# First mixture of experts: rows fetched by number from DRAM instead of by one-hot products, and a ring of 8 weight buffers instead of 6

## Chip, cores and metric

The kernel runs on 1 core of one Trainium2 chip. The metric is device time in microseconds (us) of one execution: 2,796.69 us before, the median of 3 runs (2,793.19 to 2,798.8).

## What is computed

Two blocks run one after the other: a transformer block (SwiGLU, attention, SwiGLU), and a second block of two layers, each with a mixer (gMLP, then RWKV) and a mixture of experts over 32 experts, 2 for each token. The first mixture works on 512 tokens, the second on 256. Cut to the mixture, the reference is:

```python
def hier_moe(h, w_grp, b_grp, w_exp, b_exp, w_gate, w_up, w_down):
    grp = jnp.argmax(grp_logits, axis=-1)               # best of 4 groups
    top_logit, top_idx = lax.top_k(exp_logits, TOP_K)   # 2 of its 8 experts
    weights = (p_grp * jax.nn.softmax(top_logit, axis=-1)).astype(h.dtype)
    ...
    def expert_block(args):
        xb, e = args
        return (jax.nn.silu(xb @ w_gate[e]) * (xb @ w_up[e])) @ w_down[e]
    ...
    return jnp.einsum('tk,tkd->td', weights, y)
```

All of it is float32. An expert has three matrices of 1024x512 (gate, up, down), 2 MiB each; both mixtures read all 32 experts.

## The kernel before

`moe` (L759) does a mixture. It opens a ring of weight buffers of 16 KiB a partition (`more_ring`, L771: 6 of them in the first mixture, l = 0), normalises the tokens into `h` (features down the partitions), computes the router's logits and lets `route` number the slots: expert e owns slots 64 e to 64 e + 63, and `dl` holds, token by token, the slot of its first and of its second expert. `h` is transposed tile by tile on TensorE, and the rows are kept in SBUF in two parts, `ht` high and low, whose sum is the float32 value (L808 to L811). `DB` and `WB` are slot numbers and weights of all tokens, spread over all partitions (L817, L819).

`experts` (L995) then makes 16 steps of 2 experts, 128 slots a step. Step q has these parts on TensorE:

- the gather (`gather`, L916): VectorE builds one-hot matrices `oh` of this step's slots (L923, L924), TensorE multiplies them with `ht`: 4 token tiles, 2 parts and 2 halves are 16 products `px<-hth,oh` and `px<-htl,oh` (L932); ScalarE copies the sum to `Xs` (L933); 8 transposes (L938) and 2 copies (L939) make `X`, features down;
- gate and up (L1010): 16 matmuls each, two experts side by side in the two column halves of the array; TensorE shows each float32 matmul as two records;
- `takers` and `hidden`: VectorE finds each slot's weight (L949 to L952), silu on ScalarE (L959), the product on VectorE (L960), 4 transposes (L963), a copy `hT` (L965);
- down in two halves b (L1030), 8 matmuls each, whose result is split into `y` high and low by ScalarE (L987) and VectorE (L988);
- `combine` (L974): 16 matmuls scatter `y` back to the 512 tokens, and VectorE adds them into the residuals `Rl` and `Rc` (L977): 8 feature tiles, 2 updates each, through 2 PSUM buffers `pc`.

The gather of step q + 1 is written behind gate and up of step q, but which instruction stands where on an engine is decided by a scheduler with its own estimate of times. SP issues the weights' loads in the order gate, up, down, two buffers each; a load waits until TensorE is through with what its buffer held before. `extra` (L1037) is a loop over further slots of experts with more than 64 tokens; no instruction of its body appears in the trace. Behind the first mixture stand the RWKV mixer and the second mixture (l = 1, 8 steps of 4 experts).

Of the kernel before, what the change touches and what calls it, by code (L numbers as in the profile page):

```python
# [222 lines left out]
class K:  # L223
# [529 lines left out]
    def moe(self, R, l, n, rs):  # L753

        nc, i, v = self.nc, self.i, self.nc.vector
# [11 lines left out]
        nt = n // 128  # L767
        with ExitStack() as es:

            if not l:  # L770
                es.enter_context(self.more_ring(6))  # L771
            pool = es.enter_context(self.tc.tile_pool(name=self.uid("moe"), bufs=1))
            if l:
                es.enter_context(self.more_ring(6, before=self.rings))
            ht = [pool.tile([128, nt, D], F32R, name=f"ht{j}") for j in "hl"]
            dl = pool.tile([128, 2, nt], F32, name="dl")
            ol = pool.tile([128, 2, nt], F32, name="ol")
            wt = pool.tile([128, 2, nt], F32, name="wt")
# [6 lines left out]
            with self.psum(ps=5, pt=3), self.tc.tile_pool(name=self.uid("rt"), bufs=1) as rt:  # L785
                wr = rt.tile([128, KD, 64], F32, name="wr")
                nc.scalar.dma_start(wr, i["wr"][l])
                br = rt.tile([128, 36], F32, name="br")
                nc.scalar.dma_start(br, i["br"][l].to_broadcast([128, 36]))
                h = rt.tile([128, KD, n], F32, name="h2")  # L790
                self.modulate(rt, R, l, 1, h)
                self.show(f"h2_{l}", h)
                lg = rt.tile([128, nt, 36], F32, name="lg")

                for t in range(n // SEQ):
                    p = [self.ps() for _ in range(2)]
                    for k in range(KD):
                        for j in range(2):
                            c = t * SEQ + j * 128
                            nc.tensor.matmul(p[j][:, :36], h[:, k, c:c + 128], wr[:, k, :36], start=(k == 0), stop=(k == KD - 1))  # L800
                    for j in range(2):
                        v.tensor_tensor(lg[:, 2 * t + j], p[j][:, :36], br, op=OP.add)
                self.route(rt, nt, CAPS[l], lg, dl, wt, sc, E, rk)
                for t in range(nt):
                    for b in range(2):
                        q = self.ps("pt")
                        for k in range(4):
                            nc.tensor.transpose(q[:, k * 128:(k + 1) * 128], h[:, b * 4 + k, t * 128:(t + 1) * 128], self.c("ident"))  # L808
                        hi, lo = (j[:, t, b * 512:(b + 1) * 512] for j in ht)
                        nc.scalar.activation(hi, q, AF.Copy)  # L810
                        v.tensor_tensor(lo, q, hi, op=OP.subtract)  # L811
# [77 lines left out]
    def overflow(self, pool, l, nt, sc, E, rk, ol, xinfo):  # L889
# [23 lines left out]
        v.tensor_copy(xinfo[:, :NXB], nb[0:1, 0, :NXB])  # L913
        v.tensor_copy(xinfo[:, NXB:], nb[0:1, 2, NE - 1:NE])

    def gather(self, pool, ht, dsel, nt, width):  # L916

        nc = self.nc
# [8 lines left out]
        X = pool.tile([128, KD, width], F32, tag="X", name=self.uid("X"), bufs=2)  # L927
# [6 lines left out]
        for b in range(2):  # L934
            p = self.ps("px")
            for k in range(4):
                kk = b * 4 + k
                nc.tensor.transpose(p[:, k * width:(k + 1) * width], Xs[:width, kk * 128:(kk + 1) * 128], self.c("ident", width)[:, :width])  # L938
            nc.scalar.activation(X[:, b * 4:(b + 1) * 4].rearrange("p k s -> p (k s)"), p[:, :4 * width], AF.Copy)  # L939
        return X  # L940

    def takers(self, pool, d, WB, slot, n, rows):

# [47 lines left out]
    def experts(self, R, l, n, ht, dl, DB, WB, later):  # L991
# [3 lines left out]
        cap = CAPS[l]  # L995
        G = 128 // cap
        with self.tc.tile_pool(name=self.uid("ex"), bufs=2) as pool:
            X = self.gather(pool, ht, dl, nt, 128)
            prev = None
            for q in range(NE // G):  # L1000
                last = q + 1 == NE // G
                if last:
                    self.combine(R, l, n, *prev, 128)
                pg, pu = self.ps("pg"), self.ps("pg")
                W = [[self.wtile(s[G * q + j], KD, 512) for j in range(G)] for s in (gate, up)]
                for w, p in zip(W, (pg, pu)):
# [4 lines left out]
                o, w = self.takers(pool, [DB[:, j] for j in range(2)], WB, self.c("slot")[:, q:q + 1], n, 128)  # L1011
                hT = self.hidden(pool, pg, pu, w, 128)
                if not last:
                    nc.vector.tensor_scalar(dl, dl, -128.0, None, op0=OP.add)
                    X = self.gather(pool, ht, dl, nt, 128)
                if prev is not None and not last:
                    self.combine(R, l, n, *prev, 128)
                Wd = [[], []]
# [18 lines left out]
    def extra(self, R, l, n, ht, ol, WB, xinfo, then):  # L1037
# [4 lines left out]
        def weights(name, e):  # L1042
            return self.wtile(i[name][l][bass.ds(e, 1)].rearrange("e p x -> (e p) x"), KD, 512)

        total = nc.values_load(xinfo[0:1, NXB:NXB + 1], min_val=0, max_val=NXB)
        with self.tc.tile_pool(name=self.uid("xt"), bufs=1) as pool:
            with self.tc.For_i(0, total, 1):  # L1047
                e = nc.sync.value_load(xinfo[0:1, 0:1], min_val=0, max_val=NE - 1)
                X = self.gather(pool, ht, ol, nt, cap)
                pg, pu = self.ps("pg"), self.ps("pg")  # L1050
                for name, p in (("moe_gate", pg), ("moe_up", pu)):
                    t = weights(name, e)
                    for k in range(KD):
                        nc.tensor.matmul(p[:cap], X[:, k], t[:, k], start=(k == 0), stop=(k == KD - 1))
                d = []
                for j in range(2):
                    p = self.ps("px")
                    for tt in range(nt):
                        nc.tensor.matmul(p[:, tt * 128:(tt + 1) * 128], ol[:, j, tt:tt + 1].to_broadcast([128, 128]), self.c("ident"),
                                         start=True, stop=True, skip_group_check=True)  # L1060
                    d.append(p[:cap, :n])
# [698 lines left out]
```

## Time and profile before

| | |
|---|---|
| runs before, median | 2,796.69 us |
| the profiled execution's own time | 2,806.92 us |
| its span in the trace | 2,804.9 us |
| TensorE busy over the span | 2,409.0 us (86%) |
| VectorE busy | 1,354.4 us (48%) |
| ScalarE busy | 926.2 us (33%) |
| GpSimd busy | 358.5 us (13%) |
| mean granted clock of TensorE | 0.891 |

In the profile, PE is TensorE's matmuls, PEld its weight loads, DVE VectorE, ACT ScalarE, POOL GpSimd, SP the engine that issues most transfers. L1010 is line 1010 of the kernel. A matmul row reads: line, output, inputs, shape. In brackets stands the idle time ahead of an instruction and who ended it. Times are us from the start of the span. Two consecutive rows of TensorE overlap, since matmuls are pipelined; the distance of two starts is what a group takes. The clock is a share of 2.4 GHz, so 0.50 is 1.2 GHz.

### The profile page before, as it was taken

How to read it: one execution, taken by the hardware profiler on the slowest of the kernel's cores; microseconds unless marked ns; L12 is line 12 of the kernel's file. 1: busy time of each engine (PE TensorE's matmuls, PEld its weight loads, DVE VectorE, ACT ScalarE, POOL GpSimd, SP SyncE). 2: the span in 40 equal slices, each digit the busy share in tenths (PEclk: the TensorE clock that was granted, in tenths of full speed). 3: DMA queues.
4: the chain of work that ended last, by engine and by line, in shares of the span. 5: the costliest groups of instructions: out<-in, count | busy, mean ns of one | idle time of the engine just before them, and what ended most of it. 6: DMA issues, size and time to landing. Idle time of an engine off the chain costs nothing. (4 is left out here: it accounts for less than half of the span.)

```text
span 2804.9 us, 42502 instructions
## 1 busy us (share of the span) xinstructions
PE 2409.0 (86%) x17278; PEld 1619.7 (58%) x17278; DVE 1354.4 (48%) x2792; ACT 926.2 (33%) x1715; POOL 358.5 (13%) x590
## 2 busy tenths in 40 slices
PE   7998999999999989999999959785778977767665
PEld 6986766999688865433333348664666764212211
DVE  4444754674555454443333387767776444111111
ACT  4433653543442232111111145765644222000001
POOL 0000100000200000000000022658755100000000
PEclk9999977999999979999999979797776678788887
DMA  7788720544222147899999534321110356999997
GB/s 262 261 293 293 272 79 9 202 170 170 89 98 78 73 184 302 356 360 363 363 366 370 217 104 137 96 81 45 34 46 25 120 195 264 425 424 424 425 425 292
DMA packets 174364, 616.56 MB, mean 220 GB/s; under 512 B 28035, under 2 KB 76755, under 8 KB 138835
## 3 DMA queue, kind: packets, MB, share of 16 engines
q1 hardware_dynamic: 172176, 609.66, 56.6%
q10 hardware_dynamic: 1926, 4.13, 0.4%
q8 instruction: 138, 2.26, 0.3%
q14 instruction: 60, 0.49, 0.1%
q0 software_dynamic: 64, 0.02, 0.0%
HBM read 604.15 MB, written 9.60 MB: 219 GB/s over the span
## 5 line engine op out<-in xcount | busy, mean ns | idle before, releaser
L1010 PE MATMUL pg<-w,X 128*64 128x512 f32 (+1 forms) x2048 | 451.1, 665 | 114.5 <-DMA w<-in_moe_gate_dram 58.8
L1010 PEld LDWEIGHTS pg<-w,X 128*64 128x64 f32 (+1 forms) x2048 | 116.9, 133 | 408.9 <-issue 240.7
L1097 DVE TENSOR_TENSOR wl<-w,wh 128x1024 fp32r<-128x1024 f32 (+2 forms) x208 | 249.1, 1200 | 207.5 <-ACT wh L1096 202.7
L1096 ACT ACTIVATE wh<-w 128x1024 fp32r<-128x1024 f32 (+2 forms) x208 | 215.2, 1040 | 367.7 <-PE ps L1116 310.0
L1116 PE MATMUL ps<-xs,wh 128*128 128x272 f32 (+1 forms) x1408 | 260.5, 286 | 7.3 <-DVE xs L1088 6.0
L1116 PEld LDWEIGHTS ps<-xs,wh 128*128 128x128 f32 x1408 | 219.0, 189 | 13.0 <-DVE xs L1088 7.6
L1116 PE MATMUL ps<-xs,wl 128*128 128x272 f32 (+1 forms) x704 | 200.2, 286 | 0.0
L960 DVE SCALAR_TENSOR_TENSOR hh<-hh,tw,pg 128x512 f32<-128x512 f32 x24 | 17.9, 748 | 377.0 <-PE pg L1010 377.0
L1030 PE MATMUL py<-w,hT 128*64 128x512 f32 (+1 forms) x976 | 179.7, 601 | 9.0 <-ACT hT L965 4.5
L977 DVE SCALAR_TENSOR_TENSOR Rl<-pc,mods,Rl 128x256 f32<-128x256 f32 x192 | 89.5, 480 | 179.2 <-PE pc L974 178.5
L1116 PEld LDWEIGHTS ps<-xs,wl 128*128 128x128 f32 x704 | 132.6, 189 | 1.8 <-issue 1.7
L974 PE MATMUL pc<-tk,y 128*128 128x512 f32 (+1 forms) x384 | 114.0, 397 | 18.6 <-ACT y L987 7.0
L1116 PE MATMUL ps<-hid,wh 128*128 128x272 f32 (+1 forms) x704 | 129.5, 284 | 0.0
L974 PEld LDWEIGHTS pc<-tk,y 128*128 128x128 f32 x384 | 59.4, 188 | 103.5 <-issue 51.7
L959 ACT ACTIVATE hh<-pg 128x512 f32<-128x512 f32 x24 | 14.3, 597 | 306.5 <-PE pg L1010 306.5
L1133 POOL MEMSET lora<- 64x512 f32 x4 | 2.1, 525 | 877.7 <-DVEq L1047 877.6
L1116 PEld LDWEIGHTS ps<-hid,wh 128*128 128x128 f32 x704 | 108.9, 188 | 4.2 <-issue 4.2
L1030 PEld LDWEIGHTS py<-w,hT 128*64 128x64 f32 (+1 forms) x976 | 48.8, 124 | 104.9 <-issue 86.9
L939 ACT ACTIVATE X<-px 128x512 f32<-128x512 f32 x48 | 26.6, 597 | 225.7 <-PE pg L1010 212.6
L1116 PE MATMUL ps<-hid,wl 128*128 128x272 f32 (+1 forms) x352 | 100.0, 284 | 0.0
L987 ACT ACTIVATE y<-py 128x512 fp32r<-128x512 f32 x46 | 27.5, 597 | 213.2 <-PE py L1030 198.3
L988 DVE TENSOR_TENSOR y<-py,y 128x512 fp32r<-128x512 f32 x46 | 31.7, 688 | 129.1 <-ACT y L987 129.1
(467 smaller groups left out, 4891.5 us busy)
## 6 DMA issues: line engine op xcount, KB each, us to landing
w<-in_moe_gate_dram SPq DMA_DIRECT2D x64, 2048.0 KB, 13.7
w<-in_moe_up_dram SPq DMA_DIRECT2D x64, 2048.0 KB, 18.6
w<-in_moe_down_dram SPq DMA_DIRECT2D x64, 2048.0 KB, 12.4
w<-in_ada_w_dram SPq DMA_DIRECT2D x24, 2048.0 KB, 9.1
w<-in_w_down_dram SPq DMA_DIRECT2D x16, 1408.0 KB, 6.6
w<-in_w_gate_dram SPq DMA_DIRECT2D x8, 2048.0 KB, 7.9
w<-in_w_up_dram SPq DMA_DIRECT2D x8, 2048.0 KB, 8.2
w<-in_ga_w_in_dram SPq DMA_DIRECT2D x8, 2048.0 KB, 8.4
```

What stands on the lines that cost most here:

```text
L939: nc.scalar.activation(X[:, b * 4:(b + 1) * 4].rearrange("p k s -> p (k s)"), p[:, :4 * width], AF.Copy)
L959: nc.scalar.activation(hh[:rows], pg[:rows], AF.Silu)
L960: nc.vector.scalar_tensor_tensor(hh[:rows], hh[:rows], w, pu[:rows], op0=OP.mult, op1=OP.mult)
L974: nc.tensor.matmul(p[:, :n], y[j][:rows, k * 128:(k + 1) * 128], o, start=(j == 0), stop=(j == 1))
L977: nc.vector.scalar_tensor_tensor(R[t][:, k], p[:, s], self.mod(l, 5, k, t), R[t][:, k], op0=OP.mult, op1=OP.add)
L987: nc.scalar.activation(y[0][:rows, s], p[:rows], AF.Copy)
L988: nc.vector.tensor_tensor(y[1][:rows, s], p[:rows], y[0][:rows, s], op=OP.subtract)
L1010: nc.tensor.matmul(p[a], X[:, k, a], w[j][:, k], start=(k == 0), stop=(k == KD - 1), skip_group_check=True)
L1030: nc.tensor.matmul(p[a], hT[:, k, a], Wd[b][j][:, k], start=(k == 0), stop=(k == 3), skip_group_check=True)
L1096: self.nc.scalar.activation(hi, view, AF.Copy)
L1097: self.nc.vector.tensor_tensor(lo, view, hi, op=OP.subtract)
L1116: mm(p, w[a], x[b], start=start and n == 0, stop=stop and n == 2, skip_group_check=True)
```

## The change

In the first mixture (l = 0) the rows are no longer kept in SBUF. ScalarE copies each transposed tile to `row` and writes it to a DRAM tensor `hd` of 512 rows of 4 KiB (L823, L825). For each step, `fetch` lets VectorE work out which token sits in each of the 128 slots: the slot's number is compared with `DB`, the hit is multiplied with the token's number and summed along the row (L937, twice, and L938). GpSimd then issues an indirect transfer that fetches 128 rows of `hd` into `Xs` (L940). `features` is the rest of the old gather: 8 transposes and 2 copies. The fetch for step q + 1 is written ahead of gate and up of step q; `Xs` has one buffer. A slot without a token fetches row 0; its weight is zero. The ring has 8 buffers instead of 6 there. The second mixture keeps its gather; the loop of further slots is rewritten for both.

```diff
-                es.enter_context(self.more_ring(6))
+                es.enter_context(self.more_ring(8))
...
+                        else:
+                            nc.scalar.activation(row[:, b * 512:(b + 1) * 512], q, AF.Copy)
+                    if not l:
+                        nc.scalar.dma_start(ht[t * 128:(t + 1) * 128], row)
...
+    def fetch(self, pool, hd, d, slot, n, rows):
+
+        nc, v = self.nc, self.nc.vector
+        a = pool.tile([128, n], F32, tag="tk1", name=self.uid("tk"), bufs=1)[:rows]
+        w = pool.tile([128, 4], F32, tag="tn", name=self.uid("tn"), bufs=2)[:rows]
+        x = pool.tile([128, 1], I32, tag="ti", name=self.uid("ti"), bufs=2)[:rows]
+        for j in range(2):
+            v.scalar_tensor_tensor(a, d[j], slot, self.number[:rows], op0=OP.is_equal, op1=OP.mult, accum_out=w[:, j:j + 1])
+        v.tensor_add(x, w[:, 0:1], w[:, 1:2])
+        Xs = pool.tile([128, D], F32, tag="Xs", name=self.uid("Xs"), bufs=1)[:rows]
+        nc.gpsimd.indirect_dma_start(Xs, None, hd, bass.IndirectOffsetOnAxis(ap=x, axis=0))
+        return Xs
...
-            X = self.gather(pool, ht, dl, nt, 128)
+            d = [DB[:, j] for j in range(2)]
+            X = self.gather(pool, ht, dl, nt, 128) if l else self.features(pool, self.fetch(pool, ht, d, self.c("slot")[:, 0:1], n, 128), 128)
...
+                if not l and not last:
+                    Xs = self.fetch(pool, ht, d, self.c("slot")[:, q + 1:q + 2], n, 128)
...
-                if not last:
+                if not last and l:
                     nc.vector.tensor_scalar(dl, dl, -128.0, None, op0=OP.add)
                     X = self.gather(pool, ht, dl, nt, 128)
+                elif not last:
+                    X = self.features(pool, Xs, 128)
```

What the scheduler made of it, first on SP at the start of the first mixture. Before, six weight loads stand ahead of the read of `xinfo` (the count of further slots):

```order
L1022 DMA w_9566<-in_moe_down_dram 128x2x2048
L1022 DMA w_9568<-in_moe_down_dram 128x2x2048
L1045 TENSOR_LOAD xinfo
L1045 ISA x2
L286 DMA w_9620<-in_moe_gate_dram 128x4096
L286 DMA w_9622<-in_moe_gate_dram 128x4096
```

Now eight do:

```order
L1059 DMA w_9519<-in_moe_down_dram 128x2x2048
L1059 DMA w_9521<-in_moe_down_dram 128x2x2048
L286 DMA w_9581<-in_moe_gate_dram 128x4096
L286 DMA w_9583<-in_moe_gate_dram 128x4096
L1082 TENSOR_LOAD xinfo
L1082 ISA x2
```

The gate weights of step 1 moved ahead of the read. On TensorE, in the middle of the first mixture, behind the last up matmul and the first eight gather products of a step before:

```order
L963 MATMUL pt_10727<-cst,hh_10724 128x128 x4
L932 MATMUL px_11112<-hth,oh_11087 128x512
L932 MATMUL px_11112<-htl,oh_11087 128x512
```

and, six more such products later:

```order
L938 MATMUL px_11122<-cst,Xs_11100 128x128 x4
L1030 MATMUL py_10828<-w_10822,hT_10732 64x512 x8
L938 MATMUL px_11128<-cst,Xs_11100 128x128 x4
L1010 MATMUL pg_10850<-w_10852,X_10749 64x512
L974 MATMUL pc_10958<-tk_10717,y_10826 128x512
L974 MATMUL pc_10963<-tk_10717,y_10826 128x512
L1030 MATMUL py_10839<-w_10824,hT_10732 64x512 x8
```

The rest of the `combine` is spread before between gate and up matmuls of the next step. Now, from the last up matmul of a step on:

```order
L1045 MATMUL pg_10921<-w_10928,X_10831 64x512
L995 MATMUL pt_10973<-cst,hh_10970 128x128 x4
L1067 MATMUL py_11039<-w_11033,hT_10978 64x512 x8
L1006 MATMUL pc_11142<-tk_10963,y_11037 128x512
L1006 MATMUL pc_11147<-tk_10963,y_11037 128x512
L1067 MATMUL py_11050<-w_11035,hT_10978 64x512 x8
L1006 MATMUL pc_11142<-tk_10963,y_11038 128x512
```

Thirteen more `combine` matmuls follow, and then:

```order
L951 MATMUL px_10981<-cst,Xs_10918 128x128 x4
L951 MATMUL px_10987<-cst,Xs_10918 128x128 x4
L1045 MATMUL pg_11069<-w_11071,X_10980 64x512
```

Nothing stands between the last up matmul and the transposes of `hh` any more (L995, formerly L963), and the `combine` stands in one piece behind the second down half; gate and up follow without a break. Of the 16 steps, the last 11 have this form (in 3 of them the last two `combine` matmuls stand behind the transposes of L951, and the last step of all ends with its down halves); the first 5 mix their parts.

On ScalarE, at the start, behind the copies of `DB` and `WB`, stood the copies of the first gather before:

```order
L819 ACTIVATE WB<-ps_9397 128x512
L933 ACTIVATE Xs_9424<-px_9426 128x512
L933 ACTIVATE Xs_9424<-px_9436 128x512
L939 ACTIVATE X_9425<-px_9446 128x512
L939 ACTIVATE X_9425<-px_9452 128x512
```

and now the last two of the four writes to `hd`:

```order
L823 ACTIVATE row_9357<-pt_9358 128x512
L823 ACTIVATE row_9357<-pt_9364 128x512
L825 DMA hd<-row_9357 128x1024
L823 ACTIVATE row_9371<-pt_9372 128x512
L823 ACTIVATE row_9371<-pt_9378 128x512
L825 DMA hd<-row_9371 128x1024
L952 ACTIVATE X_9425<-px_9426 128x512
```

The first transfer of L940 on GpSimd stands behind these writes. On GpSimd the 16 fetches of the first mixture stand one behind the other, with nothing between them.

## Rows read from the trace of the kernel before

**Rows 1.** Stretches of both mixtures: busy us (x instructions), clock, DMA share, GB/s.

```profile
1200.00:1250.00 50.00, 49.26 (x205) 19.22 (x202) 19.15 (x48) 5.16 (x9) 0.00 (x0) 1.00 0.90 357
...
2400.00:2500.00 100.00, 69.69 (x392) 21.95 (x392) 16.76 (x43) 8.52 (x15) 0.00 (x0) 0.82 1.01 424
```

**Rows 2.** SP's queue, 950 to 1,700 us: waits by line: us, times, longest.

```profile
SPq L286 <- PE pg L1010: 241.5, 54, 11.8
```

**Rows 3.** Timeline of TensorE, a step with the one-hot gather: start us, us, instructions.

```profile
1251.47 0.50 PE L932 MATMUL px<-hth,oh 128*128 128x512 f32 x1 [0.69 <-ACT X L939]
...
1253.44 0.60 PE L963 MATMUL pt<-cst,hh 128*128 128x128 f32 x4
1253.80 0.48 PE L932 MATMUL px<-hth,oh 128*128 128x512 f32 x1
...
1255.74 0.60 PE L938 MATMUL px<-cst,Xs 128*128 128x128 f32 x4
...
1285.95 0.50 PE L932 MATMUL px<-hth,oh 128*128 128x512 f32 x1 [0.69 <-ACT X L939]
```

**Rows 4.** Timeline of TensorE, a step without a gather.

```profile
1520.51 7.08 PE L1010 MATMUL pg<-w,X 128*64 128x512 f32 x30
1528.50 0.66 PE L963 MATMUL pt<-cst,hh 128*128 128x128 f32 x4 [0.91 <-DVE hh L960]
1529.90 3.65 PE L1030 MATMUL py<-w,hT 128*64 128x512 f32 x16 [0.75 <-ACT hT L965]
1534.25 0.74 PE L974 MATMUL pc<-tk,y 128*128 128x512 f32 x2 [0.70 <-ACT y L987]
1534.98 3.65 PE L1030 MATMUL py<-w,hT 128*64 128x512 f32 x16
1538.56 0.74 PE L974 MATMUL pc<-tk,y 128*128 128x512 f32 x2
...
1544.69 7.08 PE L1010 MATMUL pg<-w,X 128*64 128x512 f32 x30
```

**Rows 5.** Timeline of VectorE in the same step.

```profile
1539.10 0.48 DVE L977 SCALAR_TENSOR_TENSOR Rl<-pc,mods,Rl 128x256 f32<-128x256 f32 x1 [4.18 <-PE pc L974]
1539.50 0.47 DVE L977 SCALAR_TENSOR_TENSOR Rc<-pc,mods,Rc 128x256 f32<-128x256 f32 x1
...
1540.68 0.68 DVE L988 TENSOR_TENSOR y<-py,y 128x512 fp32r<-128x512 f32 x1
```

**Rows 6.** Timeline of SP's queue: reloads of the gate weights.

```profile
1070.68 0.82 SPq L286 DMA_DIRECT2D w<-in_moe_gate_dram  x2
...
1239.72 1.18 SPq L286 DMA_DIRECT2D w<-in_moe_gate_dram  x2
```

**Rows 7.** Timelines around the first and the last product of the first mixture.

```profile
1038.10 0.69 DVE L811 TENSOR_TENSOR htl<-pt,hth 128x512 fp32r<-128x512 f32 x1
...
1055.07 0.60 ACT L819 ACTIVATE WB<-ps 128x512 f32<-128x512 f32 x1 [0.30 <-PE ps L817]
...
1060.99 14.01 PE L1010 MATMUL pg<-w,X 128*64 128x512 f32 x64
...
1602.15 1.20 PE L974 MATMUL pc<-tk,y 128*128 128x512 f32 x4
```

**Rows 8.** DMA issues of the whole span: KB each, median us to landing.

```profile
raw<-in_rw_wo_dram SPq DMA_DIRECT2D x8, 512.0 KB, 3.9
...
wr<-in_wr_dram ACTq DMA_DIRECT2D x2, 256.0 KB, 9.5
...
fq<-tt POOLq DMA_DIRECT2D x1, 8.0 KB, 4.3
```

**Rows 9.** Stretches of 4 us before the first product: clock is the figure after POOL.

```profile
1040.00:1044.00 4.00, 0.28 (x2) 0.28 (x2) 3.39 (x23) 0.21 (x1) 0.00 (x0) 0.50 0.05 20
...
1052.00:1056.00 4.00, 3.31 (x21) 3.12 (x20) 3.03 (x12) 1.79 (x3) 0.00 (x0) 0.78 0.00 0
1056.00:1060.00 4.00, 4.00 (x20) 3.14 (x19) 3.77 (x11) 0.84 (x2) 0.00 (x0) 1.00 0.00 2
```

More of the change, by code (lines that the diff above doesn't have):

```diff
@@ L774, in moe @@
                 es.enter_context(self.more_ring(6, before=self.rings))
-            ht = [pool.tile([128, nt, D], F32R, name=f"ht{j}") for j in "hl"]
+            if l:
+                ht = [pool.tile([128, nt, D], F32R, name=f"ht{j}") for j in "hl"]
+            else:
+                ht = es.enter_context(self.tc.tile_pool(name=self.uid("hd"), bufs=1, space=bass.MemoryType.DRAM)).tile([n, D], F32, name="hd")
+                self.number = pool.tile([128, n], F32, name="number")
+                for t in range(nt):
+                    v.tensor_scalar(self.number[:, t * 128:(t + 1) * 128], self.c("iota"), 128.0 * t, None, op0=OP.add)
             dl = pool.tile([128, 2, nt], F32, name="dl")
@@ L804, in moe @@
                 for t in range(nt):
+                    if not l:
+                        row = rt.tile([128, D], F32, tag="row", name=self.uid("row"), bufs=2)
                     for b in range(2):
@@ L808, in moe @@
                             nc.tensor.transpose(q[:, k * 128:(k + 1) * 128], h[:, b * 4 + k, t * 128:(t + 1) * 128], self.c("ident"))
-                        hi, lo = (j[:, t, b * 512:(b + 1) * 512] for j in ht)
-                        nc.scalar.activation(hi, q, AF.Copy)
-                        v.tensor_tensor(lo, q, hi, op=OP.subtract)
+                        if l:
+                            hi, lo = (j[:, t, b * 512:(b + 1) * 512] for j in ht)
+                            nc.scalar.activation(hi, q, AF.Copy)
+                            v.tensor_tensor(lo, q, hi, op=OP.subtract)
+                        else:
+                            nc.scalar.activation(row[:, b * 512:(b + 1) * 512], q, AF.Copy)
+                    if not l:
+                        nc.scalar.dma_start(ht[t * 128:(t + 1) * 128], row)
                 for src, dst in ((dl, DB), (wt, WB)):
@@ L914, in overflow, with features @@
         v.tensor_copy(xinfo[:, NXB:], nb[0:1, 2, NE - 1:NE])
+    def fetch(self, pool, hd, d, slot, n, rows):
[9 more added lines that the diff above has]
+        return Xs
+    def features(self, pool, Xs, width):
+        nc = self.nc
+        X = pool.tile([128, KD, width], F32, tag="X", name=self.uid("X"), bufs=2)
+        for b in range(2):
+            p = self.ps("px")
+            for k in range(4):
+                kk = b * 4 + k
+                nc.tensor.transpose(p[:, k * width:(k + 1) * width], Xs[:width, kk * 128:(kk + 1) * 128], self.c("ident", width)[:, :width])
+            nc.scalar.activation(X[:, b * 4:(b + 1) * 4].rearrange("p k s -> p (k s)"), p[:, :4 * width], AF.Copy)
+        return X
     def gather(self, pool, ht, dsel, nt, width):
@@ L926, in gather @@
         Xs = pool.tile([128, D], F32, tag="Xs", name=self.uid("Xs"), bufs=1)
-        X = pool.tile([128, KD, width], F32, tag="X", name=self.uid("X"), bufs=2)
         for b in range(2):
@@ L933, in gather @@
             nc.scalar.activation(Xs[:width, b * 512:(b + 1) * 512], p[:width], AF.Copy)
[L934 to L940, printed above, removed]
+        return self.features(pool, Xs, width)
     def takers(self, pool, d, WB, slot, n, rows):
@@ L1010, in experts @@
                             nc.tensor.matmul(p[a], X[:, k, a], w[j][:, k], start=(k == 0), stop=(k == KD - 1), skip_group_check=True)
-                o, w = self.takers(pool, [DB[:, j] for j in range(2)], WB, self.c("slot")[:, q:q + 1], n, 128)
+                o, w = self.takers(pool, d, WB, self.c("slot")[:, q:q + 1], n, 128)
                 hT = self.hidden(pool, pg, pu, w, 128)
-                if not last:
+                if not last and l:
                     nc.vector.tensor_scalar(dl, dl, -128.0, None, op0=OP.add)
                     X = self.gather(pool, ht, dl, nt, 128)
+                elif not last:
+                    X = self.features(pool, Xs, 128)
                 if prev is not None and not last:
@@ L1048, in extra @@
                 e = nc.sync.value_load(xinfo[0:1, 0:1], min_val=0, max_val=NE - 1)
[L1049 to L1054, printed above, removed]
+                if l:
+                    X = self.gather(pool, ht, ol, nt, cap)
                 d = []
@@ L1060, in extra @@
                                          start=True, stop=True, skip_group_check=True)
-                    d.append(p[:cap, :n])
+                    c = pool.tile([128, n], F32, tag=f"db{j}", name=self.uid("db"))
+                    nc.scalar.activation(c, p[:, :n], AF.Copy)
+                    d.append(c[:cap])
+                if not l:
+                    X = self.features(pool, self.fetch(pool, ht, d, self.c("slot")[:cap, 0:1], n, cap), cap)
+                pg, pu = self.ps("pg"), self.ps("pg")
+                for name, p in (("moe_gate", pg), ("moe_up", pu)):
+                    t = weights(name, e)
+                    for k in range(KD):
+                        nc.tensor.matmul(p[:cap], X[:, k], t[:, k], start=(k == 0), stop=(k == KD - 1))
                 o, w = self.takers(pool, d, WB, self.c("slot")[:cap, 0:1], n, cap)
```

## The prediction, made before the changed kernel was run

> **What bounds the kernel now.** I read the stages first: busy time, clock and transfer rate stretch by stretch, to see which resource is full in the stage that is changed. In the first mixture TensorE is busy 49.26 of 50 us at full clock, while the transfers run at 357 GB/s with a busy share of 0.90 [rows 1]. The second mixture is the opposite case: TensorE busy 69.69 of 100 us, transfers at 424 GB/s with a share of 1.01. So the 357 GB/s are no ceiling: the weights have to wait. The waits of SP's queue say for whom: its weight loads stood 241.5 us in 54 waits for gate and up matmuls to let go of a buffer [rows 2]. TensorE's instructions bound this stage; a shorter TensorE step shortens it, until the transfers are full.
>
> Next, what a step is made of. From the first gather product of one step to that of the next it takes 1285.95 - 1251.47 = 34.48 us, in which TensorE idles 0.69 us [rows 3]. The whole stage, from the first gate matmul at 1060.99 to the end of the last down half at 1602.15, is 541.2 us [rows 7].
>
> The profiled execution took 2,806.92 us, 10.2 us more than the median of the runs. I make the sum on the profiled execution and take the difference over to the median.
>
> **What the change removes.** Sixteen gather products go from each step: 1253.44 - 1251.47 = 1.97 us and 1255.74 - 1253.80 = 1.94 us, together 3.9 us [rows 3]. Had nothing else moved, the step would be 34.48 - 3.9 = 30.6 us. But it was these products that stood behind the last up matmul, while VectorE and ScalarE prepared `hh` and `hT`. With the cover gone, this chain is late next, and the trace has steps near the stage's end whose gather was done earlier and that show it uncovered; one of them is [rows 4]. I build the new step from it, in the order that the changed program has:
>
> - gate and up, 64 records in one piece: 14.0 us (the row at 1060.99 [rows 7]);
> - end of up (1520.51 and 7.0) to the first down half at 1529.90: 2.4 us, the product on VectorE, 4 transposes and a copy, each waited for [rows 4];
> - down half and the wait for `y`: 1534.25 - 1529.90 = 4.35; two `combine` matmuls 0.73; second half 1538.56 - 1534.98 = 3.58 [rows 4];
> - the rest of the `combine`: 1544.69 - 1538.56 = 6.1 us [rows 4]. VectorE sets this pace, not TensorE: its 16 updates stand 0.40 us apart, with 0.6 us for `y` low between [rows 5], and TensorE has two PSUM buffers only. Before, most steps spread these matmuls among gate and up and so hid the pace; the new order puts 14 of them in one piece in each of the last 11 steps;
> - 8 transposes, two rows like the one at 1255.74 of at most 0.6 us, and what is left of the first copy to `X`: 1.4 us [rows 3].
>
> The sum is 32.5 us; in three steps two `combine` matmuls stand behind the transposes, about 0.6 us less, so 32.3 on average. The last step ends with its second down half: 14.0 + 2.4 + 3.6 + 3.6 = 23.6 us. For the first 5 steps, whose parts the new order mixes, I have two ends: 30.6 us each if the mixing fills the waits, 32.5 if not. Before, five steps took (1239.72 - 1070.68) = 169 us between reloads of the gate buffers [rows 6]. I take the middle, 31.5, as the mixed order still splits matmuls but has the same waits. Stage: 5 x 31.5 + 10 x 32.3 + 23.6 = 504 us, 37 less than 541.2.
>
> VectorE's part of the change (two comparisons with a sum and an addition in place of eight operations on `oh`) lies beside gate and up, where VectorE waits for TensorE for most of 14 us; it costs nothing as long as the numbers are there a step ahead, which the two buffers of `ti` allow.
>
> **What the change adds.** The start is a longer chain. Before, the first gate matmul began 5.3 us after the last copy of `WB` (1055.67 to 1060.99) [rows 7]. Now ScalarE has to do four copies of 0.6 us and two issues behind that copy, some 3 us; the write of 512 KB lands in about 3.9 us, as a load of that size does [rows 8]; then the fetch. No row shows an indirect fetch of 128 rows. The nearest are GpSimd's only transfer, 8 KB in 4.3 us, and a load of 512 KB in 3.9 us. One end is 3.9 us, the other is both behind one another, 8.2; I take 4.3 and the 1.2 us that 512 KB need at 424 GB/s, 5.5, nearer to the row of the same engine. With 1.4 for transposes and copy that is 13.8 us. The routing ahead gets shorter: the subtractions for `ht` low (0.69 us each [rows 7]) stood in VectorE's queue between the router's operations, and I take 2 us off. So the first gate matmul is 13.8 - 2 - 5.3 = 6.5 us later. TensorE stands idle longer here; in the stretch where it was busy 0.28 of 4 us the granted clock was 0.50, the lower of its two levels of 1.2 and 2.4 GHz, and the stretches in which it worked again show 0.78 and 1.00 [rows 9]. If the first 4 us of work run at the lower level they do the work of 2, so 2 us more. Together +8 to +9, take 8; between 4 and 14.
>
> The fetches of the other steps are not on the path as I see it: `Xs` is free when the transposes of a step are done, just ahead of its gate and up, and is wanted again 31 us later. The larger ring gives eight loads instead of six before the first matmul, and it keeps the transfers ahead of a shorter step. A step needs 12.6 MB of weights and 0.5 MB of rows, 30.9 us at 424 GB/s [rows 1]: below 32.3, but not by much. So TensorE's chain stays the bound, with transfers 96% busy.
>
> One rule speaks against this. The Trainium skill, page "SBUF — State Buffer", section "Summary: rules for kernel authors", tells authors to reckon with about 358 GB/s between HBM and SBUF. By that figure a step's 13.1 MB take 36.6 us and the change loses; the 357 GB/s of the first row seem to say the same. The trace disagrees, since the second mixture holds 424 GB/s [rows 1], and its row decides.
>
> **The rest** of the program runs the same instructions, but the scheduler puts many of those in the RWKV stage in another order: of TensorE's 5,110 instructions behind the first mixture about three in ten stand elsewhere among their neighbours. No row prices that. I take zero, give or take 8 us.
>
> Sum: -37 + 8 = -29 to -30 us. 2,806.9 - 29.7 = 2,777.2 for an execution like the profiled one, and 2,796.7 - 29.7 = 2,767 as median. The mechanism's own range, with first steps, start and the RWKV stage each at its ends, is 2,750 to 2,785.
>
> **Rivals.**
>
> 1. The waits are filled. If real delays are shorter than I stack them, the step falls to what TensorE's work alone needs, 30.6, where the transfers' 30.9 take over: 15 x 30.9 + 23.6 = 487, that is -54 + 8, and 2,750. For it: the order was made to fill gaps. Against: the uncovered waits stand in rows of this stage [rows 4].
> 2. Slower: each fetch comes late. The transfer of L940 can be issued only when `Xs` is free. If it queued behind all weights in flight (12.6 MB, 29.7 us at 424 GB/s) it would land after 29.7 + 5.5 = 35.2 us, and with the transposes' 1.2 the step would be 36.4: 15 x 36.4 + 23.6 = 570, +28 + 8, and 2,833. It decides from a fetch of some 33 us on; there 15 x 34.0 + 23.6 + 8 equals the 541 of before. Against it: the router's weights, on another queue than the expert weights, landed in 9.5 us beside six such loads [rows 8].
> 3. The transfers are the bound at the 357 GB/s that the stage shows: 88 loads and 15 fetches are 192 MB, 539 us behind the 7 us of the first gate, +5 for the last products and +8 at the start: 2,815. Against it: the share of 0.90, the waits of SP, and the 424 GB/s [rows 1, 2].
> 4. The gain is there but the RWKV stage gives it back: with 20 us or more lost to the new order, 2,787 or above. Nothing in the trace speaks for a loss rather than a gain.
>
> That the products stay is excluded for the 16 steps: the new order holds none of them in the first mixture.
>
> **Chances.** Forecast 0.68, rival 1 0.12, rival 2 0.06, rival 3 0.04, rival 4 0.10. A measurement of this kernel can tell about 0.2%, 5.6 us, from no change. Faster: nearly all of the forecast, rival 1, and most of rival 4, where the loss stays under 24 us: 0.86. Same: the last of rival 4 and the forecast's edge, 0.04. Slower: rivals 2 and 3, and losses of over 35 us in rival 4: 0.10. The range takes in rival 1 and all of rival 4 up to no change: 2,742 to 2,797.
>
> **What would show it.** No gather product in the first mixture; a step of 32 to 33 us, with idle of about 0.9 and 0.7 us ahead of the transposes of `hh` and the first down half, and VectorE named as releaser inside the piece of `combine`; the first gate matmul at 1,065 to 1,071 us; transfers above 400 GB/s; SP's waits for gate and up much shorter. A step of 31 us with share 1.0 would be rival 1; TensorE's transposes of `Xs` waiting for the transfer, rival 2. I am wrong if the stage ends no earlier than before, or if it does and the total does not follow.

## The result, and the profile of the changed kernel

The changed kernel took 2,764.89 us (median of 4 runs, 2,758.83 to 2,778.11), the kernel before 2,797.74 us beside it: a ratio of 0.9885, with a 95% interval of 0.9852 to 0.9918. A second set (6 runs against 23) gave 2,763.87 and 2,795.07 us, ratio 0.9883 (0.9849 to 0.9918). So it is faster by 32 us, about 1.2%, and the predicted 2,767 us is near. The sum behind that number is not right: one term was 14 us too good, and another, taken as zero, was a gain of 25 us. Most of what follows is about these two.

The profiled execution took 2,763.86 us, its span 2,762.1. I read it by the stages of the prediction. First the start, on TensorE's timeline (start us, us, engine, line, out<-in, count, idle before and its releaser):

```profile
1064.16 1.94 PE L951 MATMUL px<-cst,Xs 128*128 128x128 f32 x8 [12.54 <-DMA Xs<-hd,ti]
1066.03 15.79 PE L1045 MATMUL pg<-w,X 128*64 128x512 f32 x64
1081.76 1.09 PE L951 MATMUL px<-cst,Xs 128*128 128x128 f32 x8
```

GpSimd issued the first fetch at 1,058.78 us, its own row says:

```profile
1058.78 1.53 POOL L940 DMA_INDIRECT Xs<-hd,ti  x1 [316.12 <-DVE tk L937]
```

From that issue to the first transpose of the rows it is 5.4 us; the estimate was 5.5. Ahead of the issue stands a link that the prediction's chain does not have: VectorE works out the slot numbers of the first step only when the last write to `hd` has landed, 2.6 us before GpSimd issues:

```profile
1056.16 0.75 DVE L937 SCALAR_TENSOR_TENSOR tk<-DB,cst,number 128x512 f32<-128x512 f32 x1 [12.61 <-DMA hd<-row]
```

The first eight transposes took 1.94 us where later ones take 1.09, and the 64 gate and up records 15.79 instead of 13.95 us. The granted clock behind the wait was 0.50 from 1,064 to 1,068 us and 0.79 in the next 4 us; this costs 2.7 us here, 2 were forecast.

Then the step. TensorE's timeline again, one step of the later part in which the clock stays at its upper level:

```profile
1459.76 13.95 PE L1045 MATMUL pg<-w,X 128*64 128x512 f32 x64
1474.66 0.66 PE L995 MATMUL pt<-cst,hh 128*128 128x128 f32 x4 [0.95 <-DVE hh L992]
1476.06 3.65 PE L1067 MATMUL py<-w,hT 128*64 128x512 f32 x16 [0.75 <-ACT hT L997]
1480.41 0.73 PE L1006 MATMUL pc<-tk,y 128*128 128x512 f32 x2 [0.70 <-ACT y L1019]
1481.13 3.65 PE L1067 MATMUL py<-w,hT 128*64 128x512 f32 x16
1484.72 0.73 PE L1006 MATMUL pc<-tk,y 128*128 128x512 f32 x2
1486.28 1.49 PE L1006 MATMUL pc<-tk,y 128*128 128x512 f32 x4 [0.83 <-DVE Rc L1009]
1488.44 1.49 PE L1006 MATMUL pc<-tk,y 128*128 128x512 f32 x4 [0.67 <-DVE Rc L1009]
1490.20 1.49 PE L1006 MATMUL pc<-tk,y 128*128 128x512 f32 x4 [0.28 <-DVE Rc L1009]
1491.53 1.03 PE L951 MATMUL px<-cst,Xs 128*128 128x128 f32 x8
1492.81 7.52 PE L1045 MATMUL pg<-w,X 128*64 128x512 f32 x34 [0.25 <-ACT X L952]
```

This is the step that was built from [rows 4]: no gather product, waits of 0.95 and 0.75 us ahead of `hh` and the first down half, 0.70 for `y`, then VectorE (`Rc`) as the releaser inside the piece of `combine`. It takes 1492.81 - 1459.76 = 33.05 us; forecast 32.3 to 32.5. The piece from the end of the second half (1484.72) to the next gate is 8.1 us instead of 6.1 + 1.4. The 6.1 us were read off another piece. Between 1538.56 and 1544.69 in [rows 4], the kernel before has two `combine` matmuls, two gate records and these:

```profile
1540.23 1.38 PE L974 MATMUL pc<-tk,y 128*128 128x512 f32 x4
1542.29 1.49 PE L974 MATMUL pc<-tk,y 128*128 128x512 f32 x4 [0.68 <-DVE Rc L977]
1544.05 0.70 PE L974 MATMUL pc<-tk,y 128*128 128x512 f32 x2 [0.28 <-DVE Rc L977]
```

That makes 12; the last two of the step stand behind half of the next gate and up. The new piece has 14, and they take 6.8 us (1484.72 to 1491.53), with 1.3 us behind them to the gate.

But not all steps look like this one. Stretches of 4 us around an earlier step, from 1253.83 to 1290.08 (busy us of TensorE and its count, the other engines, then the granted clock, the DMA share, GB/s):

```profile
1248.00:1252.00 4.00, 2.82 (x8) 1.22 (x9) 3.81 (x10) 0.00 (x0) 0.00 (x0) 1.00 1.02 424
...
1268.00:1272.00 4.00, 2.52 (x12) 1.10 (x14) 2.75 (x7) 0.60 (x1) 0.00 (x0) 0.88 1.00 426
1272.00:1276.00 4.00, 3.48 (x12) 0.76 (x8) 0.00 (x0) 0.47 (x1) 0.00 (x0) 0.69 0.97 412
...
1280.00:1284.00 4.00, 2.63 (x10) 0.89 (x6) 2.97 (x8) 0.60 (x1) 0.00 (x0) 1.00 1.05 436
1284.00:1288.00 4.00, 3.73 (x8) 1.98 (x9) 3.34 (x9) 0.00 (x0) 0.00 (x0) 0.59 1.01 430
1288.00:1292.00 4.00, 4.00 (x16) 2.22 (x16) 3.23 (x9) 1.19 (x2) 1.19 (x1) 0.56 1.01 430
```

TensorE was busy 2.52 of 4 us around the waits for `hh` and `hT`, and the granted clock fell to 0.69; it was busy 2.63 of 4 in the piece of `combine`, and the clock fell to 0.59 and 0.56, towards 0.5, the 1.2 GHz level. In the same piece one step earlier it was busy 2.82 of 4, and the clock stayed at 1.00 until 1,268 us: the same waits do not cost the clock each time, and which of them do, no run here shows. This step took 36.2 us to the next, and its first down half 5.35 us instead of 3.65. Longer stretches of the stage, in the columns of [rows 1] and to be held against them:

```profile
1200.00:1250.00 50.00, 42.10 (x174) 15.73 (x171) 20.28 (x48) 5.38 (x9) 0.93 (x1) 0.97 1.01 425
1250.00:1300.00 50.00, 45.28 (x183) 17.31 (x184) 18.69 (x46) 5.26 (x9) 2.42 (x2) 0.90 0.95 395
...
1400.00:1450.00 50.00, 43.64 (x174) 15.68 (x172) 16.57 (x39) 4.78 (x8) 1.19 (x1) 0.90 0.90 370
```

The transfers rose from 357 to as much as 425 GB/s and TensorE's busy time fell from 49 us to 42 to 45 of 50. The prediction expected SP's waits for gate and up [rows 2] to be much shorter. They are 196.8 us in fewer and longer pieces, and the loads of the down weights now wait 85.7 us for the same matmuls, 20.9 before; eight full buffers wait for TensorE too:

```profile
SPq L286 <- PE pg L1045: 196.8, 18, 16.9
```

All stages, read off TensorE's timeline in each profiled execution, the runs of the experiments among them (in us: when the last product ahead of the first mixture, `ps<-gp`, ends; from there to the first gate matmul; first gate matmul to end of the last down half; from there to the end of the RWKV projections; from there to the first gate matmul of the second mixture; the rest; and the sum of the last five):

| run | ahead ends | start | mixture 1 | project | rest of RWKV | mixture 2, end | sum |
|---|---|---|---|---|---|---|---|
| before | 1,006.7 | 54.3 | 541.2 | 164.3 | 570.1 | 468.2 | 1,798.2 |
| before_again | 992.0 | 54.5 | 541.3 | 164.5 | 569.8 | 468.3 | 1,798.4 |
| before_afterorder | 991.8 | 54.5 | 541.2 | 164.4 | 549.6 | 470.7 | 1,780.4 |
| after_beforeorder | 992.7 | 61.5 | 515.1 | 163.9 | 562.1 | 468.6 | 1,771.2 |
| order_again | 1,024.0 | 61.1 | 517.7 | 164.3 | 559.6 | 468.7 | 1,771.4 |
| after | 1,005.9 | 60.1 | 518.2 | 164.4 | 542.4 | 471.2 | 1,756.2 |
| after_again | 1,005.6 | 60.2 | 515.6 | 163.9 | 545.0 | 471.1 | 1,755.7 |
| ring6 | 1,001.5 | 59.7 | 527.9 | 164.5 | 539.0 | 471.1 | 1,762.2 |
| spread | 997.5 | 61.6 | 475.0 | 163.6 | 548.2 | 470.8 | 1,719.3 |
| spread_ring6 | 990.2 | 58.9 | 484.1 | 163.8 | 548.0 | 471.2 | 1,725.9 |
| piece | 989.7 | 61.6 | 537.8 | 162.2 | 544.8 | 471.1 | 1,777.4 |
| filled | 1,000.7 | 61.0 | 588.7 | 168.7 | 541.6 | 471.2 | 1,831.3 |

The last column repeats to 0.5 us between executions of one program; the first does not, it moves by up to 31 us. So the comparisons below go by these stages, with the medians of many runs beside them.

### The profile page after: what moved, and what is told of

Same layout as the page of the kernel before. It is cut to its first block, busy times and chain, and to the rows that moved or that the text cites. A ratio compares the mean times of both kernels' runs of the same rounds, so it can differ in the third digit from the quotient of the medians.

```text
span 2762.1 us, 41999 instructions
## 1 busy us (share of the span) xinstructions
PE 2316.8 (84%) x17022; PEld 1558.9 (56%) x17022; DVE 1330.3 (48%) x2725; ACT 909.7 (33%) x1683; POOL 373.2 (14%) x606
## 5 line engine op out<-in xcount | busy, mean ns | idle before, releaser
L1045 PE MATMUL pg<-w,X 128*64 128x512 f32 (+1 forms) x2048 | 425.8, 666 | 115.3 <-DMA w<-in_moe_gate_dram 58.4
L992 DVE SCALAR_TENSOR_TENSOR hh<-hh,tw,pg 128x512 f32<-128x512 f32 x24 | 17.9, 747 | 445.1 <-PE pg L1045 445.1
L1006 PE MATMUL pc<-tk,y 128*128 128x512 f32 (+1 forms) x384 | 125.2, 421 | 45.6 <-DVE Rc L1009 19.8
L940 POOL DMA_INDIRECT Xs<-hd,ti x16 | 17.8, 1111 | 769.3 <-DVE tk L937 316.1
```

What stands on the lines that cost most here:

```text
L940: nc.gpsimd.indirect_dma_start(Xs, None, hd, bass.IndirectOffsetOnAxis(ap=x, axis=0))
L992: nc.vector.scalar_tensor_tensor(hh[:rows], hh[:rows], w, pu[:rows], op0=OP.mult, op1=OP.mult)
L1006: nc.tensor.matmul(p[:, :n], y[j][:rows, k * 128:(k + 1) * 128], o, start=(j == 0), stop=(j == 1))
```

## The experiments

### Where the gain behind the mixture comes from

Between the last down half and the end of the span the changed kernel gained 24.8 us (1,202.7 to 1,177.9), where the prediction had zero give or take 8. Theory A: the scheduler's other order of the RWKV stage. Rivals: the time of before in this stage was a chance of its one profiled execution (B), or what stands ahead sets the speed behind (C). To part them, everything behind the first mixture was pinned, in the changed kernel to the order of before and the other way round. The edit is the same in both, with another table:

```diff
+    def behind(self):
+        ins = [x for x in self.nc.cur_bb.bb.instructions[self.mark:] if type(x).__name__ not in SKIP]
+        last = {}
+        for n in seq:                       # place in the program -> place in the wanted order
+            x = ins[n]
+            if x.engine in last:            # order on one engine only, no wait
+                self.tc.add_manual_dep(x, last[x.engine], NoSync...)
+            last[x.engine] = x.name
```

**after_again**, the changed kernel unedited:

> The changed kernel once more, on the chip on which the next three run. Every theory: about 2,765 us; first gate matmul to last down half 518 us, last down half to the end of the span 1,178 us. How far these two stages move between two profiled executions of one program is the scale for the next three runs (2 us or less would make a difference of 10 us between orders readable).

2,763.87 us (2,759.62 to 2,771.09, 6 runs). Stages within 2.6 us of the first execution, their sum within 0.5.

**after_beforeorder**:

> The changed first mixture, but everything behind it pinned to the order of the kernel before (order only: no wait is added between engines). Theory A, the 25 us gained behind the mixture come from the scheduler's other order: mixture 518, the rest 1,193 to 1,203 instead of 1,178, total 2,780 to 2,790. Theory B, the profiled run of before was merely slow there: rest 1,178 as with the new order, total 2,765. Theory C, what stands ahead (another mixture, its clock, its buffers) sets the speed behind it: also 1,178 and 2,765; the next run parts B from C.

2,782.12 us (12 runs; ratio to before 0.9953, 0.9920 to 0.9985), 18.3 above the changed kernel. The rest of RWKV went from 542.4 and 545.0 to 562.1.

**before_afterorder**:

> The mixture of the kernel before with its gather products, but everything behind it pinned to the order of the changed kernel. Theory A (the order): mixture 541, the rest 1,178, total 2,772 to 2,782. Theory B (a slow run): 2,797, the median of before, with the rest the same as in any run of before. Theory C (what stands ahead): rest 1,195 to 1,203, total 2,797 to 2,805.

2,774.69 us (12 runs; ratio 0.9931, 0.9903 to 0.9958), 20.4 below before, and 549.6 instead of 570.1 us in the rest of RWKV.

**before_again** and **order_again**, second looks at the two programs with the old order:

> The kernel before once more, for a second profiled execution. If the order behind the mixture is what was gained: from the end of the RWKV projections to the first gate matmul of the second mixture 560 to 572 us, as in the two executions that had this order (570.1 and 562.1; the eight with the other order lie between 539.0 and 549.6). If the profiled execution of before was a chance: 540 to 550. First mixture 541 us. The work ahead of the router, the same instructions in every kernel, ends anywhere between 990 and 1,007 us.

> The changed mixture with the order of before behind it, a second profiled execution: 515 to 518 us for the first mixture, again 560 to 572 us from the projections to the second mixture if that order is the cause, 540 to 550 if not.

569.8 and 559.6 us, the second 0.4 below its range; the executions took 2,792.40 and 2,797.14 us in all. The two ends of the stage in before_again, on TensorE's timeline:

```profile
1748.09 4.17 PE L1116 MATMUL ps<-xs,ws 128*32 128x256 f32 x29
...
2322.07 3.21 PE L1010 MATMUL pg<-w,X 128*32 128x512 f32 x28
```

and in the changed kernel:

```profile
1744.42 4.18 PE L1158 MATMUL ps<-xs,ws 128*32 128x256 f32 x29
...
2290.97 3.21 PE L1045 MATMUL pg<-w,X 128*32 128x512 f32 x28
```

2322.07 - 1752.26 against 2290.97 - 1748.60: 569.8 and 542.4 us for the same instructions. B falls, since the repeat gives the old time again; A holds: the order moves this stage by 20 us with the old mixture ahead and by 15 to 20 with the new one. It costs 2.5 us in the second mixture, so 15.3 to 17.9 are left in the sum. C has a remnant: with the same order the stage is 5 to 10 us shorter behind the new mixture (562.1 and 559.6 against 570.1 and 569.8; 542.4 and 545.0 against 549.6). Its cause stays open. Pinning by itself is not what moves the stage: the five programs with the changed mixture that are pinned to the changed kernel's order have 539.0 to 548.2 us there. Which of its instructions the gain comes from was not tried.

The four sums also part the change: mixture with its start and that remnant -27.0 us under the old order (1,798.3 to 1,771.3) and -24.4 under the new, order -17.9 and -15.3, together -42.3. The medians show 31 to 33. The rest is in the work ahead of the mixture. It is the same instructions in the same order in all these programs, and it ended anywhere from 990 to 1,024 us; order_again, at 2,797.14 us in all, differs from the profiled execution of after_beforeorder (2,765.72) by nothing else. From the medians and the sums the typical execution of before ends it near 995 us (2,795.1 - 1,798.3 - 1.9 outside the span), that of the changed kernel near 1,006 (2,763.9 - 1,756.0 - 1.8). The same estimate, the median less the sum, gives 992 us for before_afterorder (12 runs), and 1,009 for after_beforeorder (12), 1,005 for spread (6) and 1,016 for ring6 (10): 10 us or more later in all four kernels with the changed mixture and six runs or more. So chance alone hardly explains it, though single executions overlap (piece 989.7, before 1,006.7). How work ahead of the mixture comes to depend on the mixture, no run here shows.

### Why the mixture gained 23 us and not 37

Theory D: VectorE's pace in the piece of `combine`, and the clock that falls in steps with that idle time. Rivals: the transfers already set the pace (E), or the clock falls for another reason (F, G, J).

**spread**: TensorE's order written by hand in the first mixture, everything behind it pinned to the changed kernel's order.

```diff
                 for m, (wj, p) in enumerate(zip(W, (pg, pu))):
                     for k in range(KD):
                         ...
+                        c = AT.get(m * KD + k)              # AT = {3: 0, 5: 1, 7: 2, 9: 3, 11: 4, 13: 5, 15: 6}
+                        if prev is not None and c is not None:
+                            self.column(R, l, n, *prev, c)      # two combine matmuls
                 ...                                             # transposes of hh
+                if prev is not None:
+                    self.column(R, l, n, *prev, 7)
                 ...                                             # first down half
+                    if not last and not b:
+                        X = turned(pool, Xs)                    # transposes of the next rows
```

> The changed kernel with TensorE's order in the first mixture written by hand, and everything behind it pinned to the changed kernel's own order: the combine matmuls of a step stand two by two among the next step's gate and up, one pair behind up and one behind the transposes of hh, and the transposes of the next rows stand between the two down halves. Theory D, the stage missed its forecast by 14 us because VectorE paces the piece of combine and because the granted clock fell in steps with that piece: steps of 29 to 31 us, clock 1.00 but for the start, stage 470 to 490 us instead of 518, total 2,717 to 2,737. Theory E, the transfers already set the pace of the steps: stage 510 to 520, total 2,757 to 2,767. Theory F, the clock falls for another reason than the idle time in that piece: the piece gone, but steps of 34 us and more still among the others, stage 485 to 500, total 2,732 to 2,747.

2,726.61 us (6 runs), ratio 0.9758 (0.9722 to 0.9793): faster than both kernels. The mixture takes 475.0 us, a step 29.8 and each of the last three 30.8 to 31.2. Its stretches, in the columns of [rows 1]:

```profile
1200.00:1250.00 50.00, 48.53 (x212) 16.27 (x210) 19.77 (x48) 5.91 (x11) 1.87 (x2) 1.00 1.01 424
1250.00:1300.00 50.00, 47.97 (x213) 16.61 (x210) 22.88 (x54) 6.33 (x11) 1.87 (x2) 1.00 1.01 424
1400.00:1450.00 50.00, 47.97 (x208) 16.60 (x208) 22.89 (x54) 6.32 (x11) 1.87 (x2) 1.00 1.01 425
```

The clock is 1.00 in every stretch from 1,100 to 1,550 us, though waits of 0.28, 0.27 and 0.46 us are left in each step. E falls: the same transfers allow a step that is 3.3 us shorter (33.05 to 29.8). Only the last three steps are held up by them: in each, one weight load on TensorE waits for its transfer, 3.0 us in all. F falls too: with the piece gone no step of 34 us is left. 37 us below the changed kernel, this is the better version of it.

**piece** and **filled** keep the piece in every step, as the changed kernel has it late in the stage; filled puts products that nobody reads into the waits (the lines with `cover` are in filled alone).

```diff
+                self.cover(X, 2)                  # ahead of the transposes of hh, and again behind them
...
+                    for c in (range(1), range(1, KD))[b]:
+                        self.cover(X, 2 if c == 0 else 1 if c > 1 else 0)
+                        self.column(R, l, n, y, o, c)
```

> TensorE's order written by hand as the changed kernel has it in its later steps, now in all 16: one combine pair behind the first down half, seven behind the second, then the transposes of the next rows. The control for the next run. Theory D, idle time in the piece of combine lets the granted clock fall: steps of 33 us at full clock and some of 34 to 36, clock of 0.90 to 0.97 in a part of the 50 us stretches, stage 520 to 540. Theory J, the clock in the changed kernel fell for something that the uneven order of its first steps brought: clock 1.00 throughout behind the start, 15 x 33.1 + 23.5, stage 518 to 523.

> The same order, but with products that nobody reads in the places where TensorE waited: two ahead of the transposes of hh, two behind them, two behind the first down half, one ahead of each combine pair from the third on (each 512 columns, 0.44 us as a gate product). They make no result earlier and cost up to 0.7 us a step where they are longer than the wait. Theory D (idle time lets the clock fall): clock 1.00 in every stretch behind the start, all steps 33 to 34 us, none of 36; stage 515 to 530 and not longer than the run before although TensorE does 12 products more in a step. Theory G, the clock falls with the work of that piece and not with its idle time: clock still below 0.97 in some stretches, steps of 36 still there, stage 8 us or more above the run before.

piece: 2,768.97 us in one run, its mixture 537.8, steps of 32.9 to 35.0, as theory D has it and not 518 to 523 (J). filled: 2,833.79 us, also in one run, its mixture 588.7, the later steps all 37.3; the expected 515 to 530 is missed by far. The cover products were priced wrongly: two of them take about 1.9 us, not 0.87. Their row shows 128*128 weights, where a gate product has 128*64:

```profile
1263.58 1.98 PE L1225 MATMUL px<-X 128*128 128x512 f32 x4
```

So filled tells nothing about the time, but it does about the clock. One stretch of each, piece first:

```profile
1350.00:1400.00 50.00, 43.30 (x180) 17.37 (x180) 21.70 (x52) 5.23 (x9) 2.17 (x2) 0.93 0.93 384
```

```profile
1350.00:1400.00 50.00, 49.50 (x198) 21.92 (x196) 21.20 (x48) 5.16 (x9) 2.23 (x2) 1.00 0.90 369
```

and TensorE's waits from 1,200 to 1,500 us (us in all, times, longest), piece:

```profile
PE pc L1150 <- DVE Rc L1153: 13.1, 26, 0.7
PE pt L1191 <- DVE hh L1188: 9.2, 9, 1.3
PE py L1206 <- ACT hT L1193: 6.7, 9, 0.7
PE pc L1150 <- ACT y L1208: 6.3, 9, 0.7
```

and filled, where no other is left:

```profile
PE pg L1185 <- ACT X L1167: 2.0, 8, 0.3
```

With the same work of `combine` and no waits the clock is 1.00 in every stretch from 1,100 to 1,650 us, with them 0.93 to 0.97 in nearly every one. So the clock goes with the idle time (D) and not with the work of the piece (G); steps of 36 us among shorter ones, as G had them, are absent.

### What the larger ring is worth

```diff
-                es.enter_context(self.more_ring(8))
+                es.enter_context(self.more_ring(6))
```

**ring6** has nothing else changed, the changed kernel's order pinned on both sides but for two loads of the loop; **spread_ring6** is spread with the same line.

> The changed kernel with six weight buffers instead of eight in the first mixture and nothing else: every instruction of every engine pinned to the changed kernel's own order, on both sides of the loop (only two weight loads for the loop itself stand a few places later on SP). Theory H, the larger ring carries nothing at this step length: a step of 33 us needs 12.6 MB of weights and 0.5 MB of rows, 30.9 us at the 425 GB/s that this stage shows, and six buffers hold one whole step: stage 515 to 522 us, total 2,760 to 2,775. Theory I, the two loads that the larger ring has ahead (4.2 MB, 9.9 us at 425 GB/s) are what lets the first steps run at 30.3 us: stage 525 to 535, total 2,770 to 2,785.

> The order written by hand with combine spread among gate and up, six buffers instead of eight. Its step is 29.8 us by TensorE's rows, below the 30.9 us that its transfers need. Theory I (the ring counts once the step is shorter than its transfers): 15 x 30.9 + 23 = 487 us and a little more, stage 485 to 500, TensorE waiting for weights in most steps. Theory H (nothing even here): 475 to 478.

ring6: 527.9 us in the mixture, 10 to 12 more than with eight buffers; 2,780.3 us as median of 10 runs, 2,765.23 to 2,803.55 (ratio to before 0.9950, 0.9916 to 0.9984). In the sum it is 6.0 to 6.5, as its rest of RWKV was 3 to 6 us shorter. Its steps settle at the same 32.4 to 35.6; the loss is at the start, where the transposes of `hh` of the first three steps stand 34.3 and 33.8 us apart instead of 23.3 and 29.4 (the early order pulls parts of later steps forward; the next distance is 34.6 in both). These are 15 us, of which the later steps give a part back. TensorE's timeline there:

```profile
1081.44 1.89 PE L1297 MATMUL pg<-w,X 128*64 128x512 f32 x2 [3.06 <-DMA w<-in_moe_gate_dram]
1087.17 3.68 PE L1297 MATMUL pg<-w,X 128*64 128x512 f32 x8 [3.83 <-DMA w<-in_moe_gate_dram]
```

Three such waits make 10.0 us; with eight buffers no weight is waited for there. Theory I holds. A scheduler that knew of six buffers might have ordered this otherwise; that was not run.

spread_ring6: 2,717.91 us in one run, its mixture 484.1 (485 to 500 expected). Its second to fourth steps take 29.8 to 29.9 us, and from the fifth on most take 30.8: there the transfers, 30.9 by their rate, set the pace. TensorE's matmul rows name only 1.3 us of waits for weights; the rest stands in the rows of its weight loads, here from 1,060 to 1,600 us (us in all, times, longest):

```profile
PEld pg L1186 <- DMA w<-in_moe_up_dram: 10.3, 11, 1.6
```

That is one wait in each of eleven steps, as theory I expected for most; spread, with eight buffers, has three of them.

## Why the prediction was right, and where not

- **The gather products went, and the waits came where the prediction put them.** 541.2 us became 515 to 518; the places and releasers of the new waits are those of [rows 4, 5].
- **The step that failed first: ten regular steps at 32.3 us.** From 1,219.95 to 1,560.86 us they took 340.9, not 323. At full clock a step is 33.05, and 32.4 where two `combine` matmuls stand behind the transposes, because the piece of `combine` to the next gate is 8.1 us and not 7.5; the 6.1 us in it were read off 12 matmuls and not 14. That is about 6 of the 18 us. The other 12 are the clock, which the prediction priced for the start alone. The step of [rows 4] has the same waits with the clock still up (its down half took 3.65 us), but the kernel before has only three such steps, and in the next one the down half already took 5.35 us (its row stands below this list). The first five steps were 153.9 us against 157.5 forecast, the last 23.3 against 23.6.
- **The ring.** The prediction gave it no term. In this order it carries 10 to 12 us of the mixture's 23 to 26, lost at the start of ring6: the 31.5 us taken for the first five steps held only with eight buffers; with six they took 33.5.
- **The start**, 6.5 us forecast to the first gate and 2 for the clock: +5.8 to the first gate from the same point ahead, 54.3 to 60.1; of the clock's 2.7 us, 1.8 lie behind it, in the mixture's column. The fetch (5.5 against 5.4) and the clock were right. Two errors cancel in the rest. The gain in the routing was taken too small: the last product with `wt` ended 4.5 us earlier after that point (43.9 against 48.4), not 2. And VectorE's slot numbers, which the prediction put at nothing, cost 2.6 us in this first step. The first gate at 1,066, inside the range given, is no evidence: it moves by 15 us between two executions of before and by 31 between after_beforeorder and order_again, which are one program.
- **The step that failed second: the RWKV stage at 0 give or take 8.** The order alone is worth 15 to 20 us there. Rival 4 had the place right and looked to the other side only.
- **Rivals 1 to 3** did not come. 1: steps of 31 us with a share of 1.0 appear in spread and spread_ring6 alone. 2: the fetches of later steps wait for `Xs` on GpSimd, and TensorE waited for a fetched row once, at the start. 3: the stage holds 424 to 426 GB/s from 1,100 to 1,250 us. The Trainium skill's 358 GB/s ("SBUF — State Buffer", "Summary: rules for kernel authors") is not the limit in any of these traces; 425 is, in spread_ring6.
- **The total.** Forecast -37 + 8 + 0 = -29; measured from the end of the work ahead, -23 + 5.8 - 25 = -42. The medians differ by 31 to 33 because, by the estimate above, the work ahead ended some 11 us later in the typical execution of the changed kernel. So two errors and a shift ahead of the mixture that no term held nearly cancel: the direction was shown beforehand, the closeness of the number is luck.

The first down half of the step behind that of [rows 4], in the kernel before:

```profile
1561.79 5.35 PE L1030 MATMUL py<-w,hT 128*64 128x512 f32 x16 [0.74 <-ACT hT L965]
```

## What to carry to other kernels

Where a scheduler orders instructions by simulated times, a change in one stage rewrites the stages behind it: compare stage by stage, and pin the order to see what is the edit's. Work that is removed from TensorE may be what covered a chain of other engines: price that chain together with the clock that its idle time costs, and then look for other work to put there, here the `combine` matmuls that VectorE had paced; that was worth more (37 us) than the whole change. A larger ring is a lead that is used up once, and does not change the steady rate: in the changed kernel it shows in the first steps, in spread it lasts for eleven steps of 29.8 us, before the transfers hold up the last three.

## What was not expected of the hardware

The work ahead of the mixture, the same instructions in the same order, took 990 to 1,024 us. The largest difference between two of these executions lies in a stretch with hardly a transfer. From 420 to 440 us (columns as above), before_again, then the changed kernel:

```profile
420.00:440.00 20.00, 17.69 (x95) 10.40 (x93) 12.65 (x51) 10.90 (x30) 1.44 (x2) 1.00 0.00 1
```

```profile
420.00:440.00 20.00, 18.71 (x57) 9.65 (x56) 8.04 (x25) 7.06 (x16) 1.45 (x2) 0.50 0.00 1
```

One execution gets the upper level and does 95 matmuls there, the other the lower and does 57. At 0.50 instead of 1.00 that stretch loses 10 us of work at the upper level, most of the 14 between the two. Why one execution is granted it and another not, no run here shows.
